# Row blocks 4 and 5 of a fused matmul and RMS norm: transposed by DMA instead of on TensorE, loaded earlier, and product 5 put first

## The chip, the cores and the metric

The kernel runs on one core of one Trainium2 chip. The metric is the device time of one execution in microseconds (us). Times are medians of repeated runs. A ratio is the mean time of one kernel's fast runs over that of the other kernel's fast runs of the same rounds, so it is not quite the ratio of the medians quoted beside it. A profile is one execution, and all times inside it count from the start of its span. The span is just under 2 us shorter than the device time.

The engines are named as the profile names them: PE is TensorE, PEld its weight loads, DVE is VectorE, ACT is ScalarE, POOL is GpSimd, and SP is SyncE, which here only issues DMAs. All DMAs of the core run on 16 DMA engines.

## The reference

```python
m, k, n = 2048, 2048, 2048      # a, b, gamma are float32
def reference(a, b, gamma, eps):
    x = np.matmul(a, b)
    rms = np.sqrt(np.mean(x ** 2, axis=-1, keepdims=True) + eps)
    return (gamma * x / rms).astype(np.float32)
```

## The kernel before

The 16 row blocks of A, 128 rows each, fall in two parts.

- **Head, blocks 0 to 3.** Two sweeps over B compute their rows directly. The first sweep takes the left half of B's columns, the second takes the right half. B comes in eight pieces per half (`b1_0` to `b1_7` for the right half); TensorE spends 14 matmuls of 216 ns, 3.02 us, on a piece, and the last group of 16 matmuls follows at the end. During the sweeps DVE builds the sums of B's quarters for the second part.
- **Groups of two blocks, 4 to 15.** Each group and half is done with seven Strassen products instead of eight, 8 matmuls (1.73 us) each. A block is loaded, its row norm is taken on ACT, it is scaled and cast to fp16, and it is transposed. For blocks 6 to 15 a DMA transposes it. For blocks 4 and 5 TensorE did that, inside the second sweep.

All large loads but three at the very start are issued by POOL and stand in one queue, here called the load queue. The DMA transposes and nearly all output stores are issued by SP.

```python
def transpose_half(mb, g):                      # blocks 4 and 5, two halves each
    bank = ps_t.tile([P, CH], FP32, name="tbank")
    view = bank.bitcast(FP16).rearrange("p (g m) -> p g m", m=P)
    for n in range(8):
        kt = g * 8 + n
        nc.tensor.matmul(view[:, n, :], a16[mb][:, kt * P:(kt + 1) * P], identity_h,
                         is_transpose=True, start=(n == 0), stop=(n == 7))
    nc.vector.tensor_copy(out=at(mb)[:, g * 8:(g + 1) * 8, :], in_=view)

def transpose_dma(mb):                          # blocks 6 to 15
    nc.sync.dma_start_transpose(at(mb), a16[mb])

# order of the load queue after the first sweep's loads (HB is 4)
later = ([("b", kp) for kp in range(5)]
         + [("a", HB), ("b", 5), ("b", 6), ("a", HB + 1), ("b", 7)])
# ... second sweep: transpose_half(4, 0), (4, 1) before the second half of steps 6 and 7,
# then in the queue:
nc.gpsimd.dma_start(out=gamma_sb, in_=gamma.partition_broadcast(P))
load_block(HB + 2)
load_block(HB + 3)
# ... last group of the sweep, with transpose_half(5, 0) and (5, 1) inside:
row_norm(HB + 2)                                # ACT, waits for block 6
a_sums(G0, (2, 5, 1))                           # DVE: A's sums for products 2, 5, 1
finish(0, (1, 0))                               # DVE scales rows of block 0, SP stores them

# first group, first half:
product(g, j, 2, p2)
nc.scalar.copy(out=c, in_=p2)                   # ACT
product(g, j, 5, p5)
nc.vector.tensor_tensor(out=t, in0=p5, in1=c, op=ALU.add)
product(g, j, 1, p1)
nc.vector.tensor_tensor(out=t, in0=p1, in1=t, op=ALU.subtract)
product(g, j, 4, p2, start=False)               # accumulates into product 2's bank
# ...
product(g, j, 3, p5, start=False)               # accumulates into product 5's bank
```

The sum for product 5 needs only block 4. The sum for product 2 needs only block 5. The tile `t` lies in the buffer of block 0's rows, so its first writing also waits for their store.

## Time and profile before

| | before |
|---|---|
| device time, median | 224.56 us |
| span of the profiled run | 222.6 us |
| PE on the chain that ended last | 83% |
| second sweep | 40.0 to 69.25 us |
| PE transposes of blocks 4 and 5 | four groups, 0.45 us of the chain each |
| DMA share, 44 to 60 us | 1.07 to 1.10 |

This is part 4 of the profile's page of the kernel before: the chain that ended last, followed back, as shares of the span by engine and then by line.

```profile
PE 83%; DMA 8%; DVE 2%; POOL 2%; issue 1%; ACT 1%; DVEq 0%; ACTq 0%; POOLq 0%
PE acc L279 63%; PE acc L350 18%; DMA b<-in_b_dram 8%; POOL early L106 1%; DVE x L617 1%; POOL b L100 1%; DVE x L620 1%; PE tbank L179 1%; PE tbank L382 1%; PE tbank L165 1%; ACT sq L291 0%; DVEq L732 0%; ACT sq L682 0%; DVE x L690 0%; DVE r L322 0%
```

TensorE is the chain. L350 is the head's matmul, L279 the products' matmul, and L179 the transposes that the change removes.

The next lines are TensorE's instructions in order of time, kernel before, from the second sweep to the first products. The columns are start (us), length (us), engine, line, operation, tiles, shapes and count. A bracket at the end would give idle time before it and what ended that.

```profile
39.84 19.80 PE L350 MATMUL acc<-b,head_at 128*128 128x512 bf16 x91
59.48 0.61 PE L179 MATMUL tbank<-identity_h,x 128*128 128x128 f16 x8
59.92 3.19 PE L350 MATMUL acc<-b,head_at 128*128 128x512 bf16 x14
...
66.65 0.61 PE L179 MATMUL tbank<-identity_h,x 128*128 128x128 f16 x8
67.09 2.32 PE L350 MATMUL acc<-b,head_at 128*128 128x512 bf16 x10
69.25 3.62 PE L279 MATMUL acc<-b,s 128*128 128x512 bf16 x16
72.70 1.89 PE L279 MATMUL acc<-t_left,s 128*128 128x512 bf16 x8
74.43 3.67 PE L279 MATMUL acc<-t_left,at_even 128*128 128x512 bf16 x16
```

No line has a bracket: TensorE never waits here. The three lines at the end are products 2 and 5 (69.25), product 1 (72.70), and products 4 and 3 (74.43).

The next view gives busy time by stretch, kernel before. After each stretch come its length, the busy us (and count) of PE, PEld, DVE, ACT and POOL, then the granted clock of TensorE, the mean busy share of the 16 DMA engines, and GB/s.

```profile
55.00:60.00 5.00, 5.00 (x31) 2.53 (x30) 4.62 (x12) 2.86 (x8) 0.54 (x1) 1.00 1.07 314
60.00:65.00 5.00, 5.00 (x33) 2.52 (x31) 4.79 (x12) 4.73 (x13) 0.53 (x1) 1.00 0.88 366
66.00:71.00 5.00, 5.00 (x31) 2.52 (x30) 4.63 (x12) 4.10 (x10) 0.00 (x0) 1.00 0.50 200
72.00:79.00 7.00, 7.00 (x34) 3.13 (x32) 6.49 (x20) 6.10 (x12) 0.00 (x0) 1.00 0.42 160
```

The DMA engines are full until about 64 us (a share over 1 is overlap of packets on one engine) and half idle after that. So the second sweep has two bounds that lie close together: TensorE, which is never idle, and the load queue, which is never empty.

### The profile page before, as it was taken

The page shows a single profiled execution, that of the slowest core. Times are in us where ns is not written, and L with a number is a line of the kernel's source. Part 1 is how long each engine was busy: PE and PEld are TensorE (multiplying, and loading weights), DVE is VectorE, ACT ScalarE, POOL GpSimd, SP SyncE. Part 2 cuts the span into 40 slices and gives each one's busy share as a digit, 9 for nine tenths or more (in the row PEclk, how much of TensorE's full clock was granted, in tenths as well). Part 3 has the DMA queues.
Part 4 walks back from the last instruction along what each step waited for, and adds up shares of the span by engine and source line. Part 5 has one row for each costly group of instructions (what it writes and reads, how often), then busy time and mean ns, then how long its engine had stood idle before and what let it go on. Part 6 is the DMA issues. An engine that isn't in the chain of part 4 may idle for free.

```text
span 222.6 us, 3026 instructions
## 1 busy us (share of the span) xinstructions
PE 211.1 (95%) x1043; PEld 98.6 (44%) x1043; DVE 161.8 (73%) x324; ACT 129.1 (58%) x272; POOL 24.5 (11%) x49
## 2 busy tenths in 40 slices
PE   7899999999999999999999999999999999999950
PEld 2445444444454444444444444444444444444430
DVE  2427557983999989978949298837994589587692
ACT  3110002807698895799646985699478954334570
POOL 7534232300000001000100002000200000000000
PEclk9999999999999999999999999999999999999997
DMA  6999999999973499818889259945994794044045
GB/s 184 223 202 209 203 208 211 212 303 259 327 280 159 188 272 292 310 72 226 276 228 400 58 174 222 366 151 143 246 368 168 97 282 189 0 188 193 0 190 188
DMA packets 36176, 47.13 MB, mean 212 GB/s; under 512 B 21952, under 2 KB 26048, under 8 KB 34496
## 3 DMA queue, kind: packets, MB, share of 16 engines
q0 software_dynamic: 9648, 23.33, 41.6%
q1 hardware_dynamic: 26080, 22.29, 33.0%
q10 hardware_dynamic: 432, 1.31, 2.0%
q8 instruction: 8, 0.13, 0.2%
q14 instruction: 8, 0.07, 0.1%
HBM read 34.60 MB, written 16.78 MB: 231 GB/s over the span
## 4 chain that ended last, share of the span: by engine, by line
PE 83%; DMA 8%; DVE 2%; POOL 2%; issue 1%; ACT 1%; DVEq 0%; ACTq 0%; POOLq 0%
PE acc L279 63%; PE acc L350 18%; DMA b<-in_b_dram 8%; POOL early L106 1%; DVE x L617 1%; POOL b L100 1%; DVE x L620 1%; PE tbank L179 1%; PE tbank L382 1%; PE tbank L165 1%; ACT sq L291 0%; DVEq L732 0%; ACT sq L682 0%; DVE x L690 0%; DVE r L322 0%
## 5 line engine op out<-in xcount | busy, mean ns | idle before, releaser
L279 PE MATMUL acc<-b,s 128*128 128x512 bf16 x376 | 83.3, 379 | 0.0
L279 PEld LDWEIGHTS <-s 128*128 128x128 f16 x472 | 46.2, 98 | 55.7 <-DVE s L244 0.2
L350 PE MATMUL acc<-b,head_at 128*128 128x512 bf16 x240 | 55.1, 379 | 0.6 <-DMA b<-in_b_dram 0.4
L291 ACT ACTIVATE sq<-x 128x512 bf16<-128x512 f32 x62 | 39.1, 631 | 10.9 <-DVE x L520 5.1
L340 DVE SCALAR_TENSOR_TENSOR x<-x,r,gamma_sb 128x1024 f32<-128x1024 f32 x28 | 34.7, 1282 | 0.8
L209 ACT ACTIVATE sq<-a 128x1024 bf16<-128x1024 f32 x24 | 25.4, 1057 | 16.8 <-DMA a<-in_a_dram 16.4
L350 PEld LDWEIGHTS <-head_at 128*128 128x128 bf16 x240 | 22.9, 98 | 26.7 <-issue 1.1
L393 ACT COPY x<-acc 128x512 f32<-128x512 f32 x11 | 5.9, 591 | 25.1 <-PE acc L350 25.1
L231 ACT ACTIVATE head_at<-a,s 128x2048 f16<-128x2048 f32 x10 | 19.9, 1990 | 0.0
L279 PEld LDWEIGHTS <-at_even 128*128 128x128 f16 x96 | 9.4, 98 | 11.5 <-issue 0.4
L279 PEld LDWEIGHTS <-head_at 128*128 128x128 f16 x96 | 9.4, 98 | 11.3
L100 POOL DMA_DIRECT2D b<-in_b_dram x15 | 10.6, 708 | 16.0 <-DMA b<-in_b_dram 13.2
L217 DVE TENSOR_SCALAR s<-norm 128x1 f32<-128x1 f32 x12 | 1.8, 150 | 14.3 <-ACT norm L212 14.2
L244 DVE TENSOR_TENSOR s<-at_even 128x1024 f16<-128x1024 f16 x15 | 9.7, 684 | 2.8 <-DMA at_even<-head_at 2.8
L291 ACT ACTIVATION_READ_ACCUMULATOR sq<-x 128x1 f32 x62 | 11.7, 188 | 0.0
L279 PE MATMUL acc<-t_left,s 128*128 128x512 bf16 x48 | 11.3, 379 | 0.0
L279 PE MATMUL acc<-early,s 128*128 128x512 bf16 x48 | 11.3, 379 | 0.0
L279 PE MATMUL acc<-early,at_even 128*128 128x512 bf16 x48 | 11.0, 379 | 0.0
L279 PE MATMUL acc<-t_left,at_even 128*128 128x512 bf16 x48 | 10.9, 379 | 0.0
L509 ACT COPY x<-acc 128x512 f32<-128x512 f32 x10 | 5.7, 575 | 8.9 <-PE acc L279 8.9
L279 PE MATMUL acc<-t_left,head_at 128*128 128x512 bf16 x48 | 10.8, 379 | 0.0
L279 PE MATMUL acc<-early,head_at 128*128 128x512 bf16 x48 | 10.8, 379 | 0.0
(86 smaller groups left out, 205.8 us busy)
## 6 DMA issues: line engine op xcount, KB each, us to landing
out_dram<-x SPq DMA_DIRECT2D x30, 512.0 KB, 3.1
a<-in_a_dram POOLq DMA_DIRECT2D x12, 1024.0 KB, 8.5
b<-in_b_dram POOLq DMA_DIRECT2D x15, 512.0 KB, 17.1
early<-in_a_dram POOLq DMA_DIRECT2D x7, 256.0 KB, 14.8
early<-in_b_dram ACTq DMA_DIRECT2D x2, 512.0 KB, 5.9
gamma_sb<-in_gamma_dram POOLq DMA_DIRECT2D x1, 1024.0 KB, 19.9
out_dram<-x SPq DMA_DIRECT2D x3, 256.0 KB, 3.5
early<-in_a_dram SPq DMA_DIRECT2D x1, 512.0 KB, 5.7
```

The lines of the kernel that those rows point to most:

```text
L100: nc.gpsimd.dma_start(out=raw[j][kp], in_=b[kp * W2:(kp + 1) * W2, j * HALF:(j + 1) * HALF].rearrange("(t p) n -> p t n", p=P))
L106: nc.gpsimd.dma_start(out=ah(kp), in_=a[0:HB * P, kp * W2:(kp + 1) * W2].rearrange("(r p) k -> p r k", p=P))
L165: nc.tensor.matmul(view[:, t, r, :], ah(kp)[:, r, t * P:(t + 1) * P], identity, is_transpose=True, start=(t == 0 and r == 0), stop=(t == 1 ...
L209: nc.scalar.activation(out=junk, in_=a32[mb][:, h * HALF:(h + 1) * HALF], func=ACTF.Square, scale=2.0 ** -8, accum_out=n2[:, h:h + 1])
L231: nc.scalar.activation(out=a16[mb], in_=a32.pop(mb), func=ACTF.Copy, scale=factor.pop(mb))
L244: nc.vector.tensor_tensor(out=s_sum[s], in0=x, in1=y, op=op)
L279: nc.tensor.matmul(bank, lhsT[:, kp, :], rhs, start=(start and kp == 0), stop=(kp == KP - 1), skip_group_check=not start)
L291: nc.scalar.activation(out=sq[:, 0:CH], in_=src, func=ACTF.Square, scale=inv_sqrt_n, accum_out=msq[mb][:, c:c + 1])
L340: nc.vector.scalar_tensor_tensor(out=x, in0=x, scalar=r, in1=gamma_sb[:, h * HALF:(h + 1) * HALF], op0=ALU.mult, op1=ALU.mult)
L350: nc.tensor.matmul(bank, head_at[:, kt, r, :], head_rhs(c, kt), start=(kt == 0), stop=(kt == KT - 1))
L393: copy(out=x_chunk(*g), in_=banks[g])
L509: nc.scalar.copy(out=x21, in_=p2)
```

## The change

The intent is to take 1.8 us of transposes off TensorE, the bound. Blocks 4 and 5 go through the DMA transpose that the other blocks use. For that they must be ready earlier, so their loads move up among B's pieces and their norms and scaling move up too. Product 5 comes first in the first group because it needs only block 4. A square root on a constant at the start brings ACT's table load forward. The diff, cut:

```diff
+    pace = consts.tile([P, 1], FP32, name="pace")
+    nc.vector.memset(pace, 1.0)
+    nc.scalar.activation(out=pace, in_=pace, func=ACTF.Sqrt)
 ...
-    def transpose_half(mb, g):                    # and identity_h
 ...
-    later = ([("b", kp) for kp in range(5)]
-             + [("a", HB), ("b", 5), ("b", 6), ("a", HB + 1), ("b", 7)])
+    later = ([("b", kp) for kp in range(3)] + [("a", HB), ("b", 3), ("b", 4), ("a", HB + 1)]
+             + [("b", kp) for kp in range(5, KP)])
 ...
+    def apply(mb):
+        row_apply(mb)
+        transpose_dma(mb)
 ...                                               # in the loop of the second sweep
-        before = [lambda: transpose_half(HB, 0)] if kp == 6 else []
-        if kp == 7:
-            before = [lambda: transpose_half(HB, 1)]
-        stream(groups2, kp, before)
+        stream(groups2, kp)
         square(squares[kp][0], x_chunk(*squares[kp]))
-        ... norm, factor and scaling of block 4 after step 4, of block 5 after step 6
+        if kp in (1, 4):
+            row_norm(HB + kp // 4)
+        b_sums_2(kp)
+        if kp in (2, 5):
+            row_factor(HB + kp // 5)
+            apply(HB + kp // 5)
 ...                                               # in the last group of the sweep
-            transpose_half(HB + 1, kt // 6)
 ...
-    a_sums(G0, (2, 5, 1))
+    a_sums(G0, (5, 2, 1))
 ...                                               # first group, first half
-        product(g, j, 2, p2)
+        one, two = (((5, p5), (2, p2)) if (g, j) == (G0, 0) else ((2, p2), (5, p5)))
+        product(g, j, *one)
-        nc.scalar.copy(out=c, in_=p2)
+        nc.scalar.copy(out=c, in_=one[1])
-        product(g, j, 5, p5)
-        nc.vector.tensor_tensor(out=t, in0=p5, in1=c, op=ALU.add)
+        product(g, j, *two)
+        nc.vector.tensor_tensor(out=t, in0=two[1], in1=c, op=ALU.add)
```

More of the change, by code (lines that the diff above doesn't have):

```diff
@@ L115, in load_block @@
         nc.gpsimd.dma_start(out=a32[mb], in_=a[mb * P:(mb + 1) * P, :])
-    pace = consts.tile([P, 1], FP32, name="pace")
     def wait_for(src):
@@ L131 @@
     nc.vector.tensor_copy(out=identity, in_=identity_f)
-    identity_h = consts.tile([P, P], FP16, name="identity_h")
-    nc.vector.tensor_copy(out=identity_h, in_=identity_f)
     warm_bank = ps_a.tile([P, CH], FP32, name="acc")
@@ L172 @@
     a16 = {}
-    def transpose_half(mb, g):
-        bank = ps_t.tile([P, CH], FP32, name="tbank")
-        view = bank.bitcast(FP16).rearrange("p (g m) -> p g m", m=P)
-        for n in range(8):
-            kt = g * 8 + n
-            nc.tensor.matmul(
-                view[:, n, :], a16[mb][:, kt * P:(kt + 1) * P], identity_h,
-                is_transpose=True, start=(n == 0), stop=(n == 7),
-            )
-        nc.vector.tensor_copy(out=at(mb)[:, g * 8:(g + 1) * 8, :], in_=view)
     def transpose_dma(mb):
@@ L414 @@
     b_sums(0, KP - 1)
-    def prepare(mb):
-        row_norm(mb)
-        row_factor(mb)
+    def apply(mb):
         row_apply(mb)
+        transpose_dma(mb)
     def b_sums_2(kp):
@@ L432 @@
         load_later(1)
-        before = [lambda: transpose_half(HB, 0)] if kp == 6 else []
-        if kp == 7:
-            before = [lambda: transpose_half(HB, 1)]
-        stream(groups2, kp, before)
+        stream(groups2, kp)
         square(squares[kp][0], x_chunk(*squares[kp]))
-        if kp == 4:
-            prepare(HB)
-        if kp == 6:
-            prepare(HB + 1)
-        elif kp == KP - 1:
-            b_sums_in_place(0, kp - 1)
-        else:
-            b_sums_2(kp)
+        if kp in (1, 4):
[4 more added lines that the diff above has]
+            apply(HB + kp // 5)
     nc.gpsimd.dma_start(out=gamma_sb, in_=gamma.partition_broadcast(P))
@@ L460 @@
     for kt in range(KT):
-        if kt in (0, 6):
-            transpose_half(HB + 1, kt // 6)
-            if kt == 0:
-                b_sums(1, KP - 2)
-                b_sum_7(1, KP - 2)
         head_matmul(bank, r3, 3, kt)
@@ L468 @@
     row_norm(HB + 2)
-    a_sums(G0, (2, 5, 1))
+    a_sums(G0, (5, 2, 1))
     finish(0, (1, 0))
-    b_sums_2(KP - 1)
     nc.scalar.copy(out=x_chunk(r3, 3), in_=bank)
@@ L542, in hook @@
             hooks[n].append(lambda: work(*args))
-        def apply(mb):
-            row_apply(mb)
-            transpose_dma(mb)
         more = g + 1 < NG
```

## The prediction

> **What bounds it now.** The chain of waits is 83% TensorE. In order of time, TensorE runs from 24.7 to 209.5 us without a gap: the second sweep over B starts at 40.0 us, the two-level products at 69.4 us, 648 of them in 140.08 us, 216 ns each. Before 24.7 us loads bound it; the last 13 us are the tail. The transposes of blocks 4 and 5 stand in this chain as four groups of eight, 0.45 us each: 1.8 us. But the second sweep has a second bound: DMA share is 1.10 from 40 to 60 us, and the DMA records say B's right pieces 3, 4, 5, 6, 7 land at 45.0, 48.6, 52.5, 56.0, 61.25 us, where TensorE needs them at 49.1, 52.1, 55.1, 58.1, 61.6. The last has 0.35 us to spare.
>
> **Removed.** 32 PE transposes (1.8 us of the chain), four DVE evictions of 0.68 us (off the chain), the 1.28 us ACT table load at 53.6 us (off the chain).
>
> **Added and moved.** Two DMA transposes. The ten existing ones keep the 16 engines for 2.62 us each; issue to landing takes 4.7 to 5.0 us. Loads do not run beside them here: three block loads begin their packets at 113.35, 137.52, 160.67 us, just after transposes end at 113.30, 137.44, 160.56. (The Trainium skill, "DMA: Bandwidth & Descriptors", section "Queues, rings and completion order", says that an engine round-robins between queues by whole packets; these records agree that the work shares one set of engines.) Bytes up to B's last piece are the same, only reordered.
>
> 1. Block 4 lands about 46, is scaled near 51.5, and its transpose moves data at about 53 to 56, in the saturated stretch. Piece 5, now behind both blocks, lands near 56 to 57.3 (needed at 55.1), piece 7 near 63 to 64 rather than 61.25.
> 2. So TensorE waits 1 to 2.2 us at piece 5 and a little at piece 7; the sweep with its last group ends at about 69 to 70.4 us (69.3 before), eating the 1.8 us or more.
> 3. Product 5 first needs only block 4, so its operand sum is in time (about 67); block 5's transpose lands near 67, in time for product 2.
> 4. The new order makes DVE's addition read product 2's bank, where product 4 accumulates; before, only an ACT copy read it. The addition waits for ACT's copy of product 5, which stands behind block 6's norm, and block 6's load is pushed by block 5's transpose to about 68 to 71 us (66.15 before). Product 4 can then wait 0 to 2.5 us.
> 5. From there nothing changes: 140 us of products and the tail.
>
> **Sum.** -1.8 (transposes) +2.0 (pieces late, 1 to 3) +0.7 (product 4, 0 to 2.5) = about +0.9 us: **225.4 us**, 8 in 10 within 222.8 to 228.3. Faster by over 2%: 0.02; within 2%: 0.92; slower by over 2%: 0.06.
>
> **What would show it.** In the waits of the second sweep, TensorE on a DMA of b, 1 to 3 us in total, longest at piece 5 or 7 (steps 1, 2). In the DMA records, the load queue thin for about 2.6 us at each transpose. On the chain near 75 us, product 4 waiting on DVE's addition (step 4). After it, gapless products.
>
> **What would make it wrong.** If transposes and loads overlap well, pieces come in time, and the time falls by up to 1.8 us (222.7). If the transposes' many 256 B packets alternate one for one with the load queue's, they land much later than 67 us, and product 2 or 5 waits for them: several us slower.

## The result, and the profile after

The changed kernel is correct and slower: 240.0 us median (four runs, 237.61 to 242.99) against 224.56 us. The ratio is 1.0661, with a 95% interval of 1.0605 to 1.0716. One of the four runs, 242.99, is slow and is not in the ratio. The profiled run is a fast one with a span of 238.7 us, 16.1 us more than before.

Part 4 of the page of the changed kernel, the chain that ended last. L267 is now the products' matmul.

```profile
PE 56%; DMA 32%; ACT 3%; DVE 3%; issue 2%; POOL 2%; DVEq 0%; ACTq 0%; POOLq 0%
PE acc L267 56%; DMA b<-in_b_dram 19%; DMA at_even<-x 12%; DMA out_dram<-x 1%; DVE x L589 1%; ACT sq L197 1%; ACT x L381 1%; POOL early L109 1%; DVE x L592 1%; ACT sq L279 1%; POOL b L103 1%; DVE x L478 0%; DVEq L704 0%; ACT sq L654 0%; DVE x L662 0%
```

A new item of 12% of the span stands in it: `DMA at_even<-x`, a DMA transpose of the scaled block. TensorE in order of time, changed kernel:

```profile
39.90 15.27 PE L338 MATMUL acc<-b,head_at 128*128 128x512 bf16 x68
56.48 6.20 PE L338 MATMUL acc<-b,head_at 128*128 128x512 bf16 x28 [1.31 <-DMA b<-in_b_dram]
63.18 6.63 PE L338 MATMUL acc<-b,head_at 128*128 128x512 bf16 x29 [0.50 <-DMA b<-in_b_dram]
80.68 6.41 PE L267 MATMUL acc<-b,s 128*128 128x512 bf16 x16 [10.86 <-DVE s L232]
86.92 1.89 PE L267 MATMUL acc<-t_left,s 128*128 128x512 bf16 x8
90.31 3.61 PE L267 MATMUL acc<-t_left,at_even 128*128 128x512 bf16 x15 [1.50 <-DVE x L478]
```

Product 4 starts at 90.31 instead of 74.43 us, 15.88 us later, and after product 3 the two profiles run alike. From the start of the next products to the end of the span it is 144.9 us after (238.7 - 93.76) and 144.7 before (222.6 - 77.94). The 15.88 us split into four parts, all read from the two lists:

| part | before | after | lost, us |
|---|---|---|---|
| end of the second sweep | 69.25 | 69.82 (80.68 - 10.86) | 0.57 |
| wait for the first product's sum | 0 | 10.86 | 10.86 |
| first two products | 3.45 | 6.24 | 2.79 |
| third product and wait for product 4 | 1.73 | 3.39 | 1.66 |

The biggest part is a wait for DVE, and DVE waits for the transpose. These are two DVE instructions of the changed kernel in order of time, the first of A's sums and the addition before product 4, then SP's issue of the two transposes:

```profile
79.93 0.69 DVE L232 TENSOR_TENSOR s<-at_even 128x1024 f16<-128x1024 f16 x1 [14.17 <-DMA at_even<-x]
89.57 0.69 DVE L478 TENSOR_TENSOR x<-acc,head_at 128x512 f32<-128x512 f32 x1 [0.97 <-DMA out_dram<-x]
51.51 27.93 SPq L174 DMA_TRANSPOSE at_even<-x  x2
```

Block 4's transpose was issued at 51.51 us, as predicted (near 51.5), and landed at 79.9. That is 28.4 us from issue to landing, where the ten transposes of the kernel before take 4.2 to 8.0. SP was held for 27.93 us to issue the two (16.08 and 11.80 us). Its issue of one used to look like this, kernel before:

```profile
77.38 2.03 SPq L186 DMA_TRANSPOSE head_at<-head_at  x1
```

The stretches, changed kernel:

```profile
55.00:60.00 5.00, 3.69 (x18) 1.63 (x17) 2.65 (x7) 3.62 (x11) 0.00 (x0) 1.00 1.14 214
60.00:65.00 5.00, 4.45 (x21) 1.97 (x21) 4.79 (x13) 1.19 (x3) 0.53 (x1) 1.00 1.01 389
66.00:71.00 5.00, 3.81 (x18) 1.55 (x16) 0.00 (x0) 0.26 (x2) 0.00 (x0) 1.00 1.30 84
72.00:79.00 7.00, 0.00 (x0) 0.00 (x0) 0.00 (x0) 0.00 (x0) 0.00 (x0) 0.55 0.95 125
```

From 66 to 79 us the DMA engines are recorded as busy as ever and move 84 to 125 GB/s. (A packet that is held up counts as busy.) Nobody else works in the last of these stretches, and TensorE's granted clock falls to 0.55.

The trace's single DMA records show what the engines did. The table counts packets that began within one microsecond, with their mean length. Loads are packets of the load queue; transposes are the 256 B packets. Packet times here count from the start of the span, like all others. Those that the prediction quotes from the packet records are 0.24 us later, so that piece 7 had about 0.6 us to spare, not 0.35; no step turns on it.

```
kernel, us      loads                      transposes
after,  57-58   92 of 2048 B, 172 ns        99, 30 ns
after,  63-64   49 of 8192 B, 310 ns        51, 18 ns
after,  67-68    9 of 8192 B, 311 ns        68, 330 ns
after,  73-74    6 of 8192 B, 318 ns        65, 94 ns
after,  80-81    0                         996, 18 ns
before, 85-86    0                         851, 22 ns
```

There are two phases. Up to 65 us the two queues take turns packet for packet: about as many transposes' packets as load packets in each microsecond, whether a load packet holds 2048 or 8192 B. One transpose is 2048 packets, so this is slow. Of block 4's 2048 packets, 700 had begun by 65 us and 1167 by 66 us. From 66 us on there is a second phase: most engines take no load packet (9 packets of 311 ns are the work of three engines), and still the transposes get only 68 and 65 packets in the two microseconds shown, with a mean length of 330 and 94 ns.

The single records show a pattern in this phase. From 66 to 69 us the load packets come in three chains without a gap: three begin at 66.04 to 66.05 us, three at 66.37 to 66.42, three at 66.69 to 66.74, and so on every 0.32 us. The transposes' packets begin in bursts at the same step: 18 at 67.00 us, 18 at 67.32, 19 at 67.65, 18 at 67.98. So they look as if all engines took one transposes' packet each and then waited for the three that were also taking loads. Thirteen load packets of block 7, as many as there are other engines, begin only at 70.96 to 71.30 us; twelve of them last 0.6 to 5.6 us instead of 0.31. All 16 landing records of block 4's transpose come within 0.32 us (79.58 to 79.90), while those of block 7's load come from 70.98 to 79.69.

### The profile page after: what moved, and what is told of

Read it like the earlier page. It is cut to its first block, busy times and chain, and to the rows that moved or that the text cites. A ratio compares the mean times of both kernels' runs of the same rounds, so it can differ in the third digit from the quotient of the medians.

```text
span 238.7 us, 2944 instructions
## 1 busy us (share of the span) xinstructions
PE 211.7 (89%) x992; PEld 97.4 (41%) x1011; DVE 159.8 (67%) x320; ACT 128.4 (54%) x272; POOL 24.5 (10%) x49
## 3 DMA queue, kind: packets, MB, share of 16 engines
q10 hardware_dynamic: 432, 1.31, 1.8%
## 4 chain that ended last, share of the span: by engine, by line
PE 56%; DMA 32%; ACT 3%; DVE 3%; issue 2%; POOL 2%; DVEq 0%; ACTq 0%; POOLq 0%
PE acc L267 56%; DMA b<-in_b_dram 19%; DMA at_even<-x 12%; DMA out_dram<-x 1%; DVE x L589 1%; ACT sq L197 1%; ACT x L381 1%; POOL early L109 1%; DVE x L592 1%; ACT sq L279 1%; POOL b L103 1%; DVE x L478 0%; DVEq L704 0%; ACT sq L654 0%; DVE x L662 0%
## 5 line engine op out<-in xcount | busy, mean ns | idle before, releaser
L267 PE MATMUL acc<-b,s 128*128 128x512 bf16 x371 | 85.8, 388 | 11.2 <-DVE s L232 10.9
L267 PEld LDWEIGHTS <-s 128*128 128x128 f16 x472 | 46.8, 99 | 68.9 <-DVE s L232 11.4
L338 PE MATMUL acc<-b,head_at 128*128 128x512 bf16 x234 | 54.3, 379 | 2.6 <-DMA b<-in_b_dram 2.2
L267 PEld LDWEIGHTS <-at_even 128*128 128x128 f16 x96 | 9.4, 98 | 13.0 <-issue 1.8
L267 PEld LDWEIGHTS <-head_at 128*128 128x128 f16 x96 | 9.4, 98 | 11.3
L267 PE MATMUL acc<-t_left,at_even 128*128 128x512 bf16 x46 | 10.7, 379 | 1.6 <-DVE x L478 1.5
L122 POOL COPY pace<-x 128x1 f32<-128x1 f32 x4 | 0.7, 183 | 105.0 <-DVE x L501 105.0
L267 PE MATMUL acc<-early,s 128*128 128x512 bf16 x46 | 11.2, 379 | 0.1
L267 PE MATMUL acc<-t_left,s 128*128 128x512 bf16 x47 | 11.1, 379 | 0.0
L267 PE MATMUL acc<-early,at_even 128*128 128x512 bf16 x48 | 10.8, 379 | 0.0
L267 PE MATMUL acc<-early,head_at 128*128 128x512 bf16 x46 | 10.7, 379 | 0.1
L267 PE MATMUL acc<-t_left,head_at 128*128 128x512 bf16 x47 | 10.6, 379 | 0.1
```

Of the source, the lines that this page charges most:

```text
L267: nc.tensor.matmul(bank, lhsT[:, kp, :], rhs, start=(start and kp == 0), stop=(kp == KP - 1), skip_group_check=not start)
L338: nc.tensor.matmul(bank, head_at[:, kt, r, :], head_rhs(c, kt), start=(kt == 0), stop=(kt == KT - 1))
```

## The experiments

Ten kernels ran. All gave correct results. In the texts, theory A is the turn by turn of packets with the load queue, and its rivals are B (the transpose is slow in itself here), C (the new load or product order costs the time) and D (the queues share by bytes or time).

### e1: nothing loads beside the transposes after B

```diff
+    wait_for(at(HB + 1)[:, 0, 0:1])      # POOL: until block 5's transpose has landed
     nc.gpsimd.dma_start(out=gamma_sb, in_=gamma.partition_broadcast(P))
     load_block(HB + 2)
     load_block(HB + 3)
```

> The changed kernel, but the loads of gamma and of blocks 6 and 7 are issued only when block 5's DMA transpose has landed. Theory A (a transpose's 128 packets per DMA engine alternate one for one with the packets of the load queue, so it crawls as long as any engine has loads queued): block 4's transpose lands near 64 to 66 us instead of 79.9, block 5's near 67 to 69, TensorE waits under 1 us for product 5 instead of 10.9 us and runs it at full clock; 240.0 - 10.9 - 2.8 = 226.3 us, plus up to 5 us because block 6's norm is now late and the addition before product 4 stands behind it: 226 to 231. Theory B (the transposes are slow by themselves in this place, because of their source or target tiles or the loads of B's pieces alone): block 4's transpose still lands after 75 us and the time stays over 236.

It took 236.28 us, ratio 1.0513 (1.0484 to 1.0542). The transposes are cured: block 4's sum was made at 65.6 us and block 5's transpose landed at 66.3. TensorE did not wait for product 5 (it began at 68.91). Rival B falls. But the total is 5 us above the range, because the gate made a new wait. This is TensorE in the second sweep and at product 4, then ACT at block 6's norm:

```profile
56.39 12.68 PE L338 MATMUL acc<-b,head_at 128*128 128x512 bf16 x58 [1.39 <-DMA b<-in_b_dram]
83.72 6.20 PE L267 MATMUL acc<-t_left,at_even 128*128 128x512 bf16 x16 [9.47 <-DVE x L479]
75.86 1.06 ACT L197 ACTIVATE sq<-a 128x1024 bf16<-128x1024 f32 x1 [7.92 <-DMA a<-in_a_dram]
```

Gamma and block 6 now land late. ACT, which works in order, stands before block 6's norm; block 0's root and the copy of product 5 stand behind it; DVE's scaling of block 0's rows and their store stand behind the root; DVE's addition stands behind all of these (it waits 0.96 us for the store at the end); and product 4 behind that. I had allowed 5 us for this chain and it was 9.5, and the two products after the wait ran slow again (6.03 instead of 3.51 us).

### e2: the new order, transposes on TensorE

```diff
-        stream(groups2, kp)
+        stream(groups2, kp, [lambda: transpose_half(HB, kp - 4)] if kp in (4, 5) else [])
 ...
     for kt in range(KT):
+        if kt in (0, 6):
+            transpose_half(HB + 1, kt // 6)
         head_matmul(bank, r3, 3, kt)
 ...  # apply(): transpose_dma only for blocks 6 and later; transpose_half and identity_h kept
```

> The changed kernel with its load order, its norm placement and product 5 first, but blocks 4 and 5 transposed on TensorE as before. Theory A: nearly all of the 15.5 us comes from the DMA transposes, so this one is within 226 to 228: no wait of 10 us before product 5, 1 to 2 us of waits for piece 5 of B, 1 to 2 us before product 4. Theory C (the load order or the product order costs most): 234 or more.

It took 225.78 us, ratio 1.0058 (1.0041 to 1.0075), just under the expected range. The DMA transposes therefore cost nearly all of the loss: the rest of the change costs 0.6%. The wait for piece 5 of B is there without any DMA transpose:

```profile
56.45 1.67 PE L351 MATMUL acc<-b,head_at 128*128 128x512 bf16 x7 [0.77 <-DMA b<-in_b_dram]
76.31 3.61 PE L280 MATMUL acc<-t_left,at_even 128*128 128x512 bf16 x16 [0.64 <-DVE x L494]
```

Piece 5 came at 56.45 us here and at 56.48 in the changed kernel. So the lateness of piece 5 comes from standing behind both blocks, as step 1 of the prediction says; the transpose beside it adds nothing that can be seen.

### e3: only the order of products, in the kernel before

The diff is the last part of the change, with `a_sums(G0, (5, 2, 1))`.

> The kernel before, with only product 5 before product 2 in the first group. Step 4 of the prediction: DVE's addition now reads the bank in which product 4 accumulates; it ended at 76.2 us, product 4 began at 74.4, so product 4 waits 1 to 2 us: 225.5 to 226.5. Rival: the order costs nothing (224.5).

It took 225.68 us, ratio 1.005 (1.0034 to 1.0067), as expected. The wait before product 4 is the one forecast:

```profile
75.96 3.61 PE L279 MATMUL acc<-t_left,at_even 128*128 128x512 bf16 x16 [1.49 <-DVE x L503]
```

### e4: only the DMA transposes, in the kernel before

```diff
-        before = [lambda: transpose_half(HB, 0)] if kp == 6 else []
-        if kp == 7:
-            before = [lambda: transpose_half(HB, 1)]
-        stream(groups2, kp, before)
+        stream(groups2, kp)
 ...  # transpose_half(HB + 1, ...) removed in the last group
         row_apply(mb)
+        transpose_dma(mb)
```

> The kernel before (its load order, product 2 first), with only the transposes of blocks 4 and 5 moved to DMA. Theory A: they are issued near 57 and 64 us, behind the same backlog of pieces and blocks, and both are needed before product 2, so that waits until about 80 to 86 us: 238 to 245 us. Theory C: without the new load order the DMA transposes cost little: under 228.

It took 235.68 us (231.97 to 243.29), ratio of the fast runs 1.0377 (1.0319 to 1.0434). Theory C falls: without any of the new order the DMA transposes cost 8 us and more. The expected range was missed: the two fast runs, 233.98 and 231.97 us, lie 4 us and more below it, because the transposes landed by 75.8 us, earlier than my 80 to 86. The other two runs (237.38 and 243.29) are slow and are not used; the median of 235.68 contains them. TensorE in the profiled run, a fast one:

```profile
55.74 11.76 PE L350 MATMUL acc<-b,head_at 128*128 128x512 bf16 x53
76.58 5.70 PE L279 MATMUL acc<-b,s 128*128 128x512 bf16 x16 [9.08 <-DVE s L244]
```

The sweep ends at 67.50 us (76.58 - 9.08), 1.75 us before that of the kernel before, with no wait for B. Here the whole saving on TensorE is to be seen, and it is lost at the next instruction.

### e5: the same backlog in four times as many loads

```diff
-    nc.gpsimd.dma_start(out=gamma_sb, in_=gamma.partition_broadcast(P))
-    load_block(HB + 2)
-    load_block(HB + 3)
+    for n in range(NCH):
+        nc.gpsimd.dma_start(out=gamma_sb[:, n * CH:(n + 1) * CH],
+                            in_=gamma[n * CH:(n + 1) * CH].partition_broadcast(P))
+    load_block(HB + 2, 4)                # four column pieces
+    load_block(HB + 3, 4)
```

> The changed kernel, but gamma and blocks 6 and 7 are each loaded as four column pieces: the same bytes, in packets of 2048 B instead of 8192 B, four times as many. Theory A (one for one by packets): while the same backlog drains, the transpose gets about four times as many turns; block 4's transpose lands by 70 to 75 us instead of 79.9, TensorE waits under 6 us before product 5 instead of 10.9, the time is 227 to 235. Theory D (the queues share by bytes or by time, or the transpose simply yields to loads): nothing changes, 79 us or later, 239 or more.

It took 242.88 us, ratio 1.0788 (1.0727 to 1.0849): the time that theory A gave was wrong. Its profiled run, at 247.61 us, is slow, so only the order of events and the packet counts are read from it. The records carry packets of 4096 B, twice as many as before rather than four times. In the first phase, at 63 us, 94 load packets of 161 ns and 111 transposes' packets began in a microsecond, against 49 and 51 in the changed kernel. Twice the load packets, twice the transposes' packets: the turns go by packet, and theory D falls for this phase. The changed kernel's own fast run says the same, with 92 and 99 beside packets of 2048 B. Block 4's transpose did land earlier, but block 5's did not:

```profile
74.36 0.69 DVE L235 TENSOR_TENSOR s<-at_even 128x1024 f16<-128x1024 f16 x1 [8.41 <-DMA at_even<-x]
88.79 1.29 DVE L235 TENSOR_TENSOR s<-at_even 128x1024 f16<-128x1024 f16 x2 [13.74 <-DMA at_even<-x]
```

Block 4's 74.4 us lies within the 70 to 75 expected, and the wait before product 5 was 5.76 us (under 6 expected). Then the last pieces of blocks 6 and 7, issued at 62.7 to 66.1 us, and block 5's transpose crawled side by side until 88 us, and product 2 waited another 10.84 us. What theory A as I had it leaves out is this second phase.

### e6: TensorE kept busy through the wait

```diff
+    idle_bank = ps_t.tile([P, CH], FP32, name="tbank")
+    for _ in range(52):
+        nc.tensor.matmul(idle_bank, raw[0][0][:, 0, 0:P], raw[0][0][:, 0, 0:CH],
+                         start=True, stop=True)
     evict(groups2[-1:], ())
```

> The changed kernel with 52 idle matmuls of 128x512 (11.2 us) put where TensorE waits for block 4's transpose. They save nothing but keep TensorE busy. If the 16 products after the wait take 6.2 us instead of 3.5 because the granted clock fell to half during the wait, they take 3.5 us now and the time falls by up to 2.7 us, to about 237.3 to 238 (less if product 4's wait for DVE's addition takes it up: then 239 to 240, and the wait before product 4 grows from 1.5 to about 4 us). If the slow products have another cause, they stay at 6.2 us.

It took 245.13 us, ratio 1.0927 (1.0876 to 1.0977), 5 us above the changed kernel's median instead of at or below it. TensorE after the idle matmuls:

```profile
82.00 3.63 PE L267 MATMUL acc<-b,s 128*128 128x512 bf16 x16 [0.64 <-DVE s L232]
85.46 1.89 PE L267 MATMUL acc<-t_left,s 128*128 128x512 bf16 x8
91.63 5.90 PE L267 MATMUL acc<-t_left,at_even 128*128 128x512 bf16 x16 [4.28 <-DVE x L482]
```

The first two products are at full speed, so the 2.79 us in the table above were the clock after the idle time. The gain was taken by the next wait, as the second half of the expectation said: product 4 now waits 4.28 us, which is 1.50 + 2.78. It is worse than neutral, because this wait is itself long enough to cost the clock: products 4 and 3 take 5.73 us (91.63 to 97.36) instead of 3.45. Products 5 and 4 both begin 1.32 us later than in the changed kernel; the last transposes' packet ended 1.1 us later in this run, which no edit explains and which I take for scatter. 1.32 us and the 2.28 us of slow clock make 3.6 us, which is the difference of the two profiled spans (3.5 us).

### e7: only block 7 held back

```diff
     load_block(HB + 2)
+    wait_for(at(HB + 1)[:, 0, 0:1])
     load_block(HB + 3)
```

> The changed kernel with only block 7's load held back until block 5's transpose has landed; gamma and block 6 are not held. Between all held (block 4's transpose landed near 63.5 us, block 5's at 66.2) and none held (79.9, 81.4). Theory A: it lands after the load queue has drained, about 68 to 71 us, block 5's about 3 us later; wait before product 5 under 2 us; total 226 to 231.

It took 232.38 us, ratio 1.0354 (1.032 to 1.0389), 1.4 us over the range. The transposes behaved as expected (block 4's landed at 70.6 us, block 5's at 72.4), product 5 began without a wait, and product 4 waited, as in e1 but less, since block 6 was not held:

```profile
57.06 14.37 PE L338 MATMUL acc<-b,head_at 128*128 128x512 bf16 x58 [2.05 <-DMA b<-in_b_dram]
71.41 3.68 PE L267 MATMUL acc<-b,s 128*128 128x512 bf16 x16
81.05 5.30 PE L267 MATMUL acc<-t_left,at_even 128*128 128x512 bf16 x16 [4.23 <-DVE x L479]
```

A second loss stands in the first line. Piece 5 came 0.6 us later than in the changed kernel, TensorE waited 2.05 us for it, and the next 58 matmuls took 14.35 us (57.06 to 71.41) where the same 58 took 12.52 in e1 (56.39 to 68.91). The granted clock was 0.60 from 57 to 60 us and 0.75 from 60 to 62. So the sweep ended at 71.41 us, 2.2 us after that of the kernel before. After the shorter waits for this piece, 1.31 us in the changed kernel and 1.39 in e1, the clock stayed whole.

### e8: an attempt to repair it

Blocks 6 and 7 are held, gamma is not; piece 5 of B goes ahead of block 5; block 0 is finished before the sums that need block 5; block 6's norm stands behind the copy of product 5.

```diff
-    ... ("b", 4), ("a", HB + 1)] + [("b", kp) for kp in range(5, KP)])
+    ... ("b", 4), ("b", 5), ("a", HB + 1)] + [("b", kp) for kp in range(6, KP)])
+    wait_for(at(HB + 1)[:, 0, 0:1])
     load_block(HB + 2)
     load_block(HB + 3)
+    take_rms(0)                                  # right after block 0's squares
-    row_norm(HB + 2)
-    a_sums(G0, (5, 2, 1))
-    finish(0, (1, 0))
+    a_sums(G0, (5,)); finish(0, (1, 0)); a_sums(G0, (2, 1))
 ...  # hooks of the first group: norm and scaling of blocks 6 and 7 later
```

> An attempt to repair the changed kernel: blocks 6 and 7 held back until block 5's transpose has landed (gamma not), B's piece 5 loaded ahead of block 5, and block 6's norm moved behind the ACT copy of product 5, with row 0 finished before the sums that need block 5. Theory A: no TensorE wait over 1 us from 40 to 90 us; the second sweep ends about 68.6 us (piece 7 bounds it, landing near 62), 0.6 us ahead of the kernel before; total 223.5 to 225.5. If waits only move elsewhere: 226 or more.

It took 244.73 us, ratio 1.0903 (1.0885 to 1.0921), 19 us over the range of theory A; the rival (waits only move elsewhere) is what happened. TensorE, ACT and TensorE again:

```profile
69.26 3.62 PE L267 MATMUL acc<-b,s 128*128 128x512 bf16 x16
78.56 1.06 ACT L197 ACTIVATE sq<-a 128x1024 bf16<-128x1024 f32 x1 [6.67 <-DMA a<-in_a_dram]
96.07 5.12 PE L267 MATMUL acc<-early,at_even 128*128 128x512 bf16 x16 [9.38 <-ACT x L476]
```

All seven products of the first half run without a wait from 69.26 us on, the aim of the repair. The sweep still waits for B by 1.13 and 0.46 us, and ends where that of the kernel before ends. But block 6, held back, kept ACT standing 6.67 us in the middle of the half. The evictions behind it came late, and the second half of the group waited 9.38 us for ACT. After that TensorE waited once more, 6.9 us, for one of A's sums. The wait was moved on, not removed.

### e9: transposes and loads never together

```diff
     # same order of pieces as e8; gamma, block 6 and block 7 held as in e1
+        if mb == HB:                             # before block 4's transpose
+            wait_for(raw[1][KP - 1][:, 1, HALF - 1:HALF])   # B's last piece has landed
+            nc.gpsimd.tensor_copy(out=a16[mb][:, 0:1], in_=a16[mb][:, 0:1])
         transpose_dma(mb)
```

> The changed kernel with B's piece 5 ahead of block 5, both DMA transposes issued only when B's last piece has landed, and gamma, block 6 and block 7 only when both transposes have landed: transposes and loads never share the engines. If the transposes beside the loads are what made B's pieces late, TensorE has no wait over 0.3 us in the second sweep and its last group ends near 67.8 us, 1.5 us before that of the kernel before: here the 1.8 us saved would show. Each transpose then moves its data in 2.6 to 2.8 us, block 4's landing near 66, block 5's near 69. It must be paid after: gamma and block 6 land 8 to 10 us later than in the kernel before, product 4 waits about 10 us for the addition behind them, total 234 to 238. Rival: the sweep still ends near 69.3, so the reordered loads alone use up the gain.

It took 239.24 us, ratio 1.0667 (1.0648 to 1.0685). The loads ended at 61.0 us, and the two transposes ran one after the other from 64.2 to 69.3 us, 2.6 and 2.5 us, 841 packets of 22 ns in the microsecond from 65 us. TensorE:

```profile
58.82 9.66 PE L338 MATMUL acc<-b,head_at 128*128 128x512 bf16 x44 [0.62 <-DMA b<-in_b_dram]
68.31 1.89 PE L267 MATMUL acc<-b,s 128*128 128x512 bf16 x8
86.39 6.00 PE L267 MATMUL acc<-t_left,at_even 128*128 128x512 bf16 x16 [12.19 <-DVE x L485]
```

The sweep ends at 68.3 us, 0.94 us ahead of the kernel before. That lies between my two expectations: the new order costs a 0.62 us wait even with nothing beside the loads, and most of the rest of the saving is there. It is paid for with 12.19 us before product 4, because gamma and block 6 now come after both transposes; that wait is 2 us longer than expected, and the total 1.2 us over the range.

### e10: only the early table load, in the kernel before

The diff is the first part of the change.

> The kernel before with only the early square root on ACT, which brings the table load of 1.28 us from 53.6 us to the start. Off the chain: same time, within 0.3%.

It took 224.19 us against 224.45, ratio 0.999 (0.9978 to 1.0003): the same, as expected.

### What they say together

The end of the last transposes' packet follows the end of the loads that stood beside them, from the DMA records of each profiled run:

```
kernel   first packet of   last load packet    last packet of
         the transposes    beside them         block 5's transpose
e1          55.2 us           61.8 us              65.8 us
e8          55.2              65.0                 68.0
e7          55.2              69.1                 71.9
e4          60.8              73.6                 75.3
e6          55.7              78.8                 82.0
after       55.4              79.1                 80.9
e5 (slow)   55.5              88.1                 88.2
e9          64.2          (none beside them)       69.3
```

In seven kernels the transposes began within 6 us of each other and ended 0.1 to 4.0 us after the loads, be that 62 or 88 us. That is the main finding: in none of these kernels did the transposes end before the loads beside them had ended. The turn by turn of packets accounts for the first phase, as the changed packet size of e5 shows. For the second phase no run tests the mechanism. The bursts at the step of the load packets, and the 16 landing records within 0.32 us, fit a transpose whose packets go out to the 16 engines in step, so that the engines that also take loads set the pace for all. The same step would give one transposes' packet for one load packet in the first phase too, so the two phases may be one mechanism. But the records carry no engine numbers, the step is not strict (in e4 two of the 16 landing records of block 4's transpose came 2.8 us after the others), and it may come from SP's issue, which was held all the while, and not from the transpose. It stays an inference. Why most of block 7's packets began only at 71 us is not known either.

The loads suffer in turn. Block 7, the last in the load queue, took its packets from 67.3 to 79.1 us in the changed kernel and 65.7 to 70.7 in the kernel before (counted as the last 128 packets).

## Why the prediction was wrong

- **What bounds it: right.** e4 shows it most clearly. With the transposes gone and the old load order kept, the sweep ended 1.75 us earlier, the predicted 1.8.
- **Step 1, first half: wrong, and this is the step that failed.** "Its transpose moves data at about 53 to 56, in the saturated stretch." It was issued at the time predicted, began at 55.4, and landed at 79.9. I took 2.62 us from ten transposes during which no load packet began, and took three loads that began just after a transpose had ended for a sign that the transpose has the engines to itself. Those records show only what happens when the transpose is there first. In the other order the packets took turns, and then the transposes did not end before the loads. How the second half of that came about is open, as said above.
- **Step 1, second half, and step 2: right.** TensorE waited 1.31 us at piece 5 and 0.50 at piece 7, and the sweep with its last group ended at 69.8 us (69 to 70.4 forecast). e2, without these DMA transposes, has piece 5 at the same time, as the stated cause (its place behind both blocks) asks. It has no wait at piece 7, which it needs at about 62.9 us; in the changed kernel the piece came at 63.18. So a small part of that lateness may come from the transposes beside it.
- **Step 3: wrong as a consequence.** Product 5 waited 10.86 us. Adding the two lines of the table that the prediction had no term for, this wait and the 2.79 us of slow clock after it, gives 13.65 of the 15.88 us.
- **Step 4: right in size and place, not in the last link.** Product 4 waited for the addition, 1.50 us (0 to 2.5 forecast), and 1.49 in e3 alone. But in the changed kernel the addition did not wait last for ACT's copy of product 5, which was done by 87.5 us, nor did the norm wait for block 6's load, which landed at 68.67 us (68 to 71 forecast): ACT itself was held by the transposes until 80 us. The addition waited 0.97 us, until 89.57, for the store of block 0's rows, whose root stands behind block 6's norm. That the size still fits is in part luck.
- **Step 5: right.** 144.9 against 144.7 us from there to the end.
- **"What would make it wrong" named the event,** one for one alternation, but gave it "several us" and little weight. A sum that warns of it could have been made beforehand: 2048 packets on 16 engines are 128 turns each, and a turn beside a load packet costs 173 ns (B) or 310 ns (blocks) by the records of the kernel before. As an estimate, 128 turns need 22 to 40 us of full queue, and in the kernel before that queue was full until about 64 us and had block 7 still to come. The sum warns, but it does not give the 79.9 us: the turns fill the ten microseconds to 65 us, and most of the delay fell in the second phase, which it doesn't contain.

On what the pages state: the Trainium skill, "DMA: Bandwidth & Descriptors", section "Queues, rings and completion order", says that an engine round-robins between queues packet by packet. The first phase agrees (92 and 99, 49 and 51, and in e5 94 and 111 in a microsecond). The prediction named this sentence and still gave the transpose the engines to itself for 2.6 us in its sum, leaving the turns to what would make it wrong. "TensorE: Matmul & The Clock Gate", section "What's actually happening", says that the clock halves after an idle window of about 3.4 us and comes back after a similar one of work. This case agrees: after waits of 10.86, 9.47 and 4.28 us the next two products took 6.24, 6.03 and 5.73 us instead of 3.45 to 3.51. But e7 shows the halved clock after a wait of 2.05 us, shorter than that window.

## What to carry to other kernels

A DMA transpose that lands 4.2 to 8.0 us after its issue with no loads beside it took 28.4 us beside a full load queue. Count its packets as turns behind the other queue's packets, and look at when that queue is empty before moving a transpose there. A stage where TensorE and the loads are both at their limit has no cheap place for work taken from TensorE: 1.8 us of PE were exchanged for 5.2 us of DMA, and each order tried for them (e1, e7, e8, e9) only moved the wait to the next consumer of a load. And a wait of a few microseconds that is moved costs more than itself, because the clock falls: 2.79, 2.28 and 1.8 us were lost so in the changed kernel, e6 and e7.

## What the Trainium skill lacked or had wrong

- "DMA: Bandwidth & Descriptors", section "Rules for kernel authors", says of a transpose next to ordinary DMAs that it "needs nothing". That holds for the result, which was correct in every run here. It lacks the time: 28.4 us from issue to landing beside a full load queue against 4.2 to 8.0 us in the kernel before.
- The same page gives an effective bandwidth for DMA transposes (section "Latency and other measured facts") without saying that it is lost beside loads. Here the 16 engines together moved 84 GB/s at a busy share of 1.30 while block transposes and loads were both in flight.
- The same section says that two of the engines are usually slower than the others with loads issued from GpSimd. No run here shows which engine is which. At 67 us three engines' worth of load packets ran while the others took none, and the transposes' packets began only at the step of these, 0.32 us. No page says that a few engines with loads can hold up a whole transpose; here it is an inference from the records.
- "TensorE: Matmul & The Clock Gate" was right that the clock halves after idle time; that was missing from my sum (2.79 us), not from the page. Its idle window of about 3.4 us is not the shortest wait that costs the clock: in e7 a wait of 2.05 us was enough, and 58 matmuls took 14.35 us instead of 12.52.
